# Attention scores of a two-layer hybrid trunk: float32r parts on the whole array, three score banks, stepwise gate products

## The chip, the cores and the metric

The kernel runs on one core of a Trainium2 chip. The metric is the device time of one execution in microseconds (us): the median of three runs, and for the profile the one execution that the hardware profiler recorded. Engines are named as in the profile: PE is TensorE's matmul row and PEld its weight loads, DVE is VectorE, ACT ScalarE, POOL GpSimd, SP SyncE (which only issues transfers).

## What is computed

Two layers work on 2048 latent tokens (a 32 x 64 grid) and 256 context tokens, 1024 wide, all in float32. One layer, cut to what matters here:

```
h   = rms_norm(x) * (1 + scale) + shift
p   = h @ w_in                                  # 3104 columns, split over four groups
a   = gated linear attention, both directions, chunks of 64 (4 heads)
b   = 2-D Fourier mixing @ w_f
c   = windowed attention: 4 query heads, 2 key heads, 3 blocks of 128 + 256 context keys + a sink
d   = neighbourhood attention on the grid: 4 heads, 8 x 16 window with a bias + 256 context keys
y   = concat(group * silu(its gate)) @ w_out
x   = x + gate * y                              # context tokens too, in layer 0
```

For c and d, q and k are normalized per head (c also rotated); scores are q.k over 64 dimensions, plus a mask or bias, then a softmax over local and context keys together.

## The kernel before, in words

The kernel is written for a planner: the program gives instructions in a logical order, with priorities, and the planner puts them on the engines' queues by its own costs; every queue then runs in order. Tokens come in 9 subs of 256 (sub 0 is context), and tiles of 128.

*Projections* (`project`, `mm3`). A float32 product is made of three float32r products: both operands are split into a high part, which is the value rounded to float32r, and a low part, the rest. One projection of a sub to 256 columns is 2 x 8 x 3 matmuls of 128 x 256. Weights are loaded by SP (L211) and split by ACT (L212) and DVE or POOL (L213). `norm_x` and `prep_h` do the same for the tokens; `norm_x` uses the PSUM bank `ph` for two small matmuls.

*q and k* (`normrope`, `store_t`). For the chunks cq, dq, dk (four heads) and ckv (two heads of k) the projection is squared (L358), multiplied by the norm's weight out of PSUM (L362), scaled and for the window heads rotated, transposed by TensorE into the bank `ph` (L327), copied out by ACT and stored to scratch in HBM, float32, with the 64 dimensions as rows.

*GLA* (`gla_fast`) runs beside the projections; its score tile for four heads is read out as 2, 1 and 1 heads. Its outputs use the bank `py`.

*Attention* (`attention`, `pipeline`, `swa`, `na`, `na_ctx_rows`). The work is a list of items, one for each head and block of 128 queries: 272 items in the two layers (176 with 640 keys, 64 with 768, 32 shorter). `load_q` brings q from scratch by SP, twice, once to rows 0 to 63 and once to rows 64 to 127 (four slots), since in `attend` the local keys lie on rows 0 to 63 and the context keys on rows 64 to 127, each multiplied on its half of the array in float32 (L816). The scores of one item fill the only tile of the pool `pS`, two PSUM banks. One DVE instruction adds the bias or mask, stores the negated scores and takes their extremum (L822); ACT takes the exponential and its sum (L830); `transpose_p` transposes blocks of 128 keys by TensorE into one of the two banks of `pm` (L848), DVE copies the first three blocks out (L858) and ACT the rest (L856); L908 multiplies by the values for a pair of heads into `py`, and DVE multiplies by the reciprocal sums (L911). Two small copies on POOL belong to it: the sink column behind the scores (L826) and the reciprocal sums of a pair, spread over columns for a transpose (L851). The bias of a neighbourhood head comes by SP into one tile for each of the two heads of a pair (L998). Keys come by POOL's queue (`na_keys` and `prep` of `swa`, L1023 to L1027 and L926), five items ahead.

*Output* (`prep_mix`, `out_proj`). A half of a sub's group outputs and its gates (`scr_y`, `scr_g`) are loaded to y (one buffer) and g, multiplied on DVE (L1069), and split (L1070, L1071); out_proj then is 4 x 48 matmuls a sub. In `attention` such a call is an item of its own in the list: when it is reached, the products of all its subs are put at high priority, and the matmuls behind them.

*Banks.* PSUM's eight banks: `pp` two (projections), `pS` two, `pm` two, `py` one, `ph` one.

## Time and profile before

| | us |
|---|---|
| median of 3 runs | 2973.59 |
| lowest, highest | 2966.96, 2979.63 |
| profiled execution | 2984.5 |
| its span, first to last instruction | 2982.7 |
| PE busy in the span | 2727.1 (91%) |
| DVE busy | 1596.8 (54%) |
| ACT busy | 1044.7 (35%) |
| POOL busy | 808.7 (27%) |

Matmuls overlap, so a busy PE is not PE at its peak. Attention lies from about 915 to 1560 us (layer 0) and from 2389 to 2925 us (layer 1); projections and GLA before, with the Fourier mixing and the backward GLA scan between; at the end stand the last output projections.

### The profile page before, as it was taken

What the parts mean: (1) busy time and instruction counts of PE and PEld (TensorE: products, weight loads), DVE (VectorE), ACT (ScalarE), POOL (GpSimd) and SP (SyncE); (2) the same over time, 40 slices, a digit from 0 to 9 for tenths busy, and PEclk for the clock granted to TensorE, in tenths of its full rate; (3) what the DMA queues carried; (4) which work ended last, traced back from release to release, by engine and by line L of the source; (5) the groups of instructions that cost most, each with busy time, mean ns of one, the idle gap of its engine ahead of it and who ended that gap; (6) DMA issues with size and microseconds to landing.
All of it is one profiled execution on the core that took longest, in us unless ns stands there. A gap on an engine that the chain in (4) does not pass through costs nothing. (4 is left out here: it accounts for less than half of the span.)

```text
span 2982.7 us, 55851 instructions
## 1 busy us (share of the span) xinstructions
PE 2727.1 (91%) x21206; PEld 2404.4 (81%) x21206; DVE 1596.8 (54%) x3730; ACT 1044.7 (35%) x2322; POOL 808.7 (27%) x911
## 2 busy tenths in 40 slices
PE   5999999999789989989998998999997988898988
PEld 5989999999767657758787988989986866585868
DVE  7556444587663655453747454346339446545453
ACT  2333342343222543342443333323432235324342
POOL 3234323323441111111413333234126211111212
PEclk9999999999889999999999999999998999899999
DMA  7523443363645735364444465233327475455535
GB/s 248 175 92 101 144 132 92 111 220 122 180 139 162 208 100 173 108 162 140 142 136 154 145 197 170 89 94 127 115 83 209 123 198 157 121 168 150 176 108 161
DMA packets 430921, 434.95 MB, mean 146 GB/s; under 512 B 54059, under 2 KB 309805, under 8 KB 430253
## 3 DMA queue, kind: packets, MB, share of 16 engines
q1 hardware_dynamic: 427022, 417.59, 46.0%
q0 software_dynamic: 3616, 13.64, 1.8%
q8 instruction: 172, 2.82, 0.4%
q14 instruction: 111, 0.91, 0.1%
HBM read 328.03 MB, written 103.07 MB: 145 GB/s over the span
## 5 line engine op out<-in xcount | busy, mean ns | idle before, releaser
L220 PE MATMUL ps<-whi,hh 128*128 128x256 f32 x1968 | 578.4, 294 | 28.7 <-DVE nsq L362 21.7
L222 PE MATMUL ps<-whi,hl 128*128 128x256 f32 x1968 | 572.5, 291 | 6.9 <-DVE hl L259 5.2
L221 PE MATMUL ps<-wlo,hh 128*128 128x256 f32 x1968 | 572.4, 291 | 6.9 <-PEq L625 6.0
L213 POOL TENSOR_TENSOR wlo<-wraw,whi 128x512 fp32r<-128x512 f32 x208 | 283.8, 1364 | 855.4 <-ACT whi L212 828.4
L220 PEld LDWEIGHTS ps<-whi,hh 128*128 128x128 f32 x1968 | 385.5, 196 | 40.9 <-DVE nsq L362 13.8
L212 ACT CAST whi<-wraw 128x512 fp32r<-128x512 f32 x416 | 243.0, 618 | 486.9 <-DMA wraw<-w_in 221.2
L220 PE MATMUL ps<-hh,whi 128*128 128x256 f32 x1376 | 404.0, 294 | 8.9 <-DVE nsq L362 5.9
L221 PE MATMUL ps<-hl,whi 128*128 128x256 f32 x1376 | 399.7, 291 | 0.0
L222 PE MATMUL ps<-hh,wlo 128*128 128x256 f32 x1376 | 398.8, 290 | 0.0
L221 PEld LDWEIGHTS ps<-wlo,hh 128*128 128x128 f32 x1968 | 385.6, 196 | 9.9 <-issue 6.3
L222 PEld LDWEIGHTS ps<-whi,hl 128*128 128x128 f32 x1968 | 385.4, 196 | 9.1 <-DVE hl L259 6.6
L220 PE MATMUL pso<-mh,whi 128*128 128x256 f32 x1088 | 319.0, 294 | 9.5 <-ACT mh L1070 5.8
L222 PE MATMUL pso<-mh,wlo 128*128 128x256 f32 x1088 | 316.7, 292 | 4.0 <-POOL wlo L213 2.8
L221 PE MATMUL pso<-ml,whi 128*128 128x256 f32 x1088 | 316.5, 291 | 0.0
L830 ACT ACTIVATE S<-S,am 128x641 f32<-128x641 f32 (+5 forms) x272 | 226.4, 832 | 190.4 <-DVE am L822 173.0
L816 PE MATMUL pse<-kst,q 64*128 64x256 f32 (+2 forms) x1184 | 257.5, 476 | 36.6 <-DVE am L822 32.6
L213 DVE TENSOR_TENSOR wlo<-wraw,whi 128x512 fp32r<-128x512 f32 x208 | 192.6, 931 | 182.2 <-ACT whi L212 174.5
L848 PE MATMUL ppt<-idn,S 128*128 128x128 f32 x1360 | 237.7, 294 | 54.5 <-DVE pt L858 42.4
L220 PEld LDWEIGHTS ps<-hh,whi 128*128 128x128 f32 x1376 | 269.9, 196 | 16.8 <-DVE nsq L362 7.2
L848 PEld LDWEIGHTS ppt<-idn,S 128*128 128x128 f32 x1360 | 153.9, 146 | 150.5 <-issue 45.7
L222 PEld LDWEIGHTS ps<-hh,wlo 128*128 128x128 f32 x1376 | 269.2, 196 | 5.0 <-issue 4.8
L221 PEld LDWEIGHTS ps<-hl,whi 128*128 128x128 f32 x1376 | 269.6, 196 | 3.2 <-issue 2.7
(200 smaller groups left out, 4817.4 us busy)
## 6 DMA issues: line engine op xcount, KB each, us to landing
wraw<-w_in SPq DMA_DIRECT2D x288, 256.0 KB
wraw<-w_out SPq DMA_DIRECT2D x128, 256.0 KB
adaw<-ada_w SPq DMA_DIRECT2D x82, 256.0 KB
scr_g<-ev SPq DMA_DIRECT2D x68, 256.0 KB
g<-scr_g SPq DMA_DIRECT2D x34, 512.0 KB
y<-scr_y SPq DMA_DIRECT2D x34, 512.0 KB
bias<-nbias SPq DMA_DIRECT2D x48, 256.0 KB
brec<-scr_so SPq DMA_DIRECT2D x34, 321.0 KB
```

The source lines that it names most:

```text
L212: nc.scalar.copy(hi[:, k], raw)
L213: (nc.gpsimd if i % 4 else nc.vector).tensor_tensor(out=lo[:, k], in0=raw, in1=hi[:, k], op=ALU.subtract)
L220: nc.tensor.matmul(out, ah(k), bh(k), start=(k == 0), stop=False)
L221: nc.tensor.matmul(out, ah(k), bl(k), start=False, stop=False)
L222: nc.tensor.matmul(out, al(k), bh(k), start=False, stop=(k == KB - 1))
L816: nc.tensor.matmul(p[:, lo:hi], q[r], k, start=True, stop=True, tile_position=(64 * o, 0))
L830: nc.scalar.activation(out=S[:, 0:w], in_=S[:, 0:w], func=AF.Exp, scale=-1.0, bias=m[:, 0:1], accum_out=m[:, 1:2])
L848: nc.tensor.transpose(p[:, i], S[:, (c0 + i) * 128:(c0 + i + 1) * 128], self.idn)
```

## The change

- `store_t` becomes `split_t`: the transposed q or k is split out of PSUM, the high part by ACT as a rounding copy, the low part by DVE as a subtraction, and both are stored. The transposes now use the bank of `py`; the pool `ph` is gone, and the small matmuls of `norm_x` move to `pm`.
- Keys are loaded with the high part on rows 0 to 63 and the low part on rows 64 to 127, local and context keys alike. q's high part lies on both halves of the rows, and its low part, in another tile, too. A score block is then two float32r matmuls over 128 rows, accumulated: (high q) x (high and low k), (low q) x (high and low k).
- Loads of q and k convert from float32 to float32r and go by POOL's queue. For a pair of neighbourhood heads one transfer brings both parts of both heads, with the 64 source rows read twice; for a block of the window heads there are four.
- The scores of two consecutive heads lie in one tile of three banks: the first head's local keys end at column 512 and its context keys follow, the second head's context keys start at 768 and its local keys at 1024. The order of probability blocks and values of the second head changes with it.
- Two bias tiles for each head of a pair, used in turn.
- In `attention` the gate products of three calls of out_proj are steps behind later items: at each step, two items apart, one half is multiplied and the next is loaded, and out_proj's matmuls follow the last one. A product is pinned behind what is already in DVE's order, and goes into g, not y. The other out_proj calls, and the gate projections, are put behind the last item of the phase ahead of them.
- The copies of the transposed probabilities of a pair's first head are all on DVE, those of the second all on ACT.
- GLA's score tile is read out as 3 heads and 1.

```diff
@@ Kern.build, norm_x
-            self.ph = ctx.enter_context(tc.tile_pool(name="ph", bufs=1, space=PSUM))
...
-        p1 = self.ph.tile([128, 512], F32, tag="h", name="p1")
+        p1 = self.pm.tile([128, 512], F32, tag="m", name="p1")
@@ store_t -> split_t
-        p = self.ph.tile([128, 2, 256], F32, tag="h", name="pst")
+        p = self.py.tile([128, 2, 256], F32, tag="y", name="pst")
...
-        x = self.ev.tile([128, 2, 256], F32, tag="sq", name="th")
+        hi = self.ev.tile([128, 2, 256], F32R, tag="sq", name="th")
+        lo = self.ev.tile([128, 2, 256], F32R, tag="e", name="tl")
...
-            nc.scalar.copy(x[:, 0:n], p[:, 0:n])
+            nc.scalar.copy(hi[:, 0:n], p[:, 0:n])
+            nc.vector.tensor_tensor(out=lo[:, 0:n], in0=p[:, 0:n], in1=hi[:, 0:n], op=ALU.subtract)
+        for l, x in zip(range(2), (hi, lo)):
+            x = x.bitcast(F32)
+            if name == "cq":
+                nc.sync.dma_start(self.sqc[l].rearrange("(i p) t -> p i t", p=128)[:, :, tok], x)
+            elif name == "ckv":
+                nc.sync.dma_start(self.skc[:, l, :, tok], x[:, 0])
+            elif name == "dk":
                 for i in range(2):
+                    nc.sync.dma_start(self.skd[2 * i:2 * i + 2, l, :, tok], x[:, i])
...
@@ gla_fast
-                for h0, n in ((0, 2), (2, 1), (3, 1)):
+                for h0, n in ((0, 3), (3, 1)):
@@ loads
-    def load_q(self, pool, src, n):
-        q = pool.tile([128, n, 128], F32, tag="q", name="q", bufs=4, padded_shape=[128, 4, 128])
-        for o in range(2):
-            self.nc.sync.dma_start(q[64 * o:64 * o + 64], src)
-        return q
+    def load_k(self, pool, dst, src, h0, t0, n):
+        src = src[h0:h0 + 2].rearrange("h l d t -> (l d) h t")
+        self.nc.gpsimd.dma_start(dst[:, :, 0:n], src[:, :, t0:t0 + n])
+    def load_q(self, pool, src):
+        q = pool.tile([128, 2, 2, 128], F32R, tag="q", name="q", bufs=4)
+        self.nc.gpsimd.dma_start(q.rearrange("p h l t -> p (h l t)"), src.rearrange("d h l t -> d (h l t)").rearrange("(o d) x -> o d x", o=1).to_broadcast([2, 64, 512]))
+        return q[:, :, 0], q[:, :, 1]
+    def load_q4(self, pool, src):
+        out = []
+        for d in range(2):
+            q = pool.tile([128, 4, 128], F32R, tag="q", name="q", bufs=4)
+            for o in range(2):
+                self.nc.gpsimd.dma_start(q[64 * o:64 * o + 64], src(d))
+            out.append(q)
+        return out
@@ attend
-        p = self.pS.tile([128, 1024], F32, tag="s", name="pse")
-        for o, lo, hi, k in parts:
-            r = slice(64 * o, 64 * o + 64)
-            nc.tensor.matmul(p[:, lo:hi], q[r], k, start=True, stop=True, tile_position=(64 * o, 0))
+        n, a0 = nloc + 256, 768 if side else 512 - nloc
+        p = self.S3
+        for lo, hi, k in ((1024, 1024 + nloc, kloc), (768, 1024, kc)) if side else ((a0, 512, kloc), (512, 768, kc)):
+            if hi > lo:
+                nc.tensor.matmul(p[:, lo:hi], qa[:, h], k, start=True, stop=False)
+                nc.tensor.matmul(p[:, lo:hi], qb[:, h], k, start=False, stop=True)
@@ transpose_p
-            if c0:
+            if rc is not None:
                 nc.scalar.copy(pt[:, 0:w], p[:, 0:w])
             else:
                 nc.vector.tensor_copy(out=pt[:, 0:w], in_=p[:, 0:w])
@@ kv_tiles (new, in place of na_keys)
+        kc = pool.tile([128, 2, 256], F32R, tag="kc", name="kc", bufs=2)
+        self.load_k(pool, kc, kt, h0, 0, 256)
+        kst = None
+        if n:
+            kst = pool.tile([128, 2, 1024], F32R, tag="kst", name="kst", bufs=2)
+            self.load_k(pool, kst, kt, h0, t0, n)
@@ na
+            b = pool_st["b", i]
             if cg != 2:
-                if ("b", i) not in pool_st:
...
+                b.insert(0, b.pop())
@@ prep_mix
-    def prep_mix(self, L, s):
+    def prep_mix(self, L, subs, late=False):
...
+        def product(s, c):
+            g, y = got.pop(0)
+            hh, hl = mix[s]
+            ins = nc.vector.tensor_tensor(out=g, in0=y, in1=g, op=ALU.mult)
+            if late:
+                self.tc.keep_in_program_order(ins)
+            nc.scalar.copy(hh[:, :, c], g)
+            (nc.gpsimd if c.start else nc.vector).tensor_tensor(out=hl[:, :, c], in0=g, in1=hh[:, :, c], op=ALU.subtract)
...
+        def step(k):
+            if k > 0:
+                product(*halves[k - 1])
+            if k < len(halves):
+                load(*halves[k])
@@ attention
+            self.S3 = self.pS.tile([128, 1536], F32, tag="s", name="pse")
+            for i in range(2):
+                self.bias["b", i] = [p.tile([128, 768], F32, name=f"bias{i}{x}", bufs=1) for x in range(2)]
...
+                n = 2 * len(subs)
+                for k in range(1, n + 1):
+                    behind.setdefault(at + 2 * k, []).append(lambda k=k: out.steps[k]())
+                behind.setdefault(at + 2 * n, []).append(lambda: self.out_proj(L, subs, mix))
@@ trunk
-                self.attention(L, 3, 2, g, [10, 11, 12, 13, 14, 15], 0, f(T3), [-2, -1, 0, 1, 2, 3], None, 1, f(T1), [4, 5, 6, 7, 8, 9])
+                self.attention(L, 3, 2, g, [10, 11, 12, 13, 14, 15], 0, ("out", T3), [-2, -1, 0, 1, 2, 3], None, 1, ("out", T1), [4, 5, 6, 7, 8, 9])
...
-                self.attention(L, 3, 2, g, [10, 11, 12, 13, 14, 15], 0, f(T3), [0, 1, 2, 3], 1, [4, 5], [6, 7], [8, 9], f(T1), f([3, 4]), f([5]))
+                self.attention(L, 3, 2, g, [10, 11, 12, 13, 14, 15], 0, ("out", T3), [0, 1, 2, 3], 1, [4, 5], [6, 7], [8, 9], f(T1), f([3, 4]), f([5]))
```

## Rows read from the trace of the kernel before

**Rows 1.** Page: busy us of each engine, share of the span, instructions.

```profile
PE 2727.1 (91%) x21206; PEld 2404.4 (81%) x21206; DVE 1596.8 (54%) x3730; ACT 1044.7 (35%) x2322; POOL 808.7 (27%) x911
```

**Rows 2.** Windows by stage: start:end, length, busy us of each engine, PEclk, DMA share, GB/s.

```profile
100.00:750.00 650.00, 632.76 (x5027) 606.36 (x5026) 368.25 (x829) 227.26 (x492) 201.79 (x164) 0.99 0.43 136
915.00:1560.00 645.00, 587.92 (x4753) 465.76 (x4751) 336.22 (x829) 247.66 (x592) 122.42 (x232) 0.95 0.51 147
1560.00:2250.00 690.00, 650.32 (x5090) 623.70 (x5089) 339.95 (x733) 238.37 (x498) 224.04 (x182) 0.98 0.43 135
2389.00:2925.00 536.00, 483.72 (x3959) 372.78 (x3958) 277.81 (x673) 214.24 (x513) 91.61 (x188) 0.94 0.54 154
```

**Rows 3.** Page: the chain that ended last, shares of the span by line.

```profile
PE py L908 2%; PE pse L816 2%; PE ppt L848 2%; DMA y<-scr_y 2%; PE pso L220 2%; PE pso L222 1%; PE pso L221 1%; DMA bias<-nbias 1%; DMA wraw<-w_out 1%; DMA scr_y<-yt 1%; ACT S L830 1%; DVE S L822 1%; PE pab L726 1%; PE ps L220 1%; PE ps L22
```

**Rows 4.** Waits of the whole span: engine and line <- releaser, us in total, times, longest.

```profile
DVE y L1069 <- DMA y<-scr_y: 84.7, 29, 8.6
...
PE ppt L848 <- DVE pt L858: 42.4, 15, 5.7
...
POOL kst L1023 <- PE pse L816: 36.5, 10, 6.4
...
PE pse L816 <- DVE am L822: 32.6, 61, 3.9
...
PE ps L220 <- DVE nsq L362: 27.7, 18, 6.9
...
DVE S L822 <- DMA bias<-nbias: 22.3, 10, 5.3
```

**Rows 5.** Timeline of three short stretches, TensorE: start us, us, engine, line, operation, tiles.

```profile
2639.51 0.30 PEld L816 LDWEIGHTS pse<-kst,q 64*128 64x128 f32 x4 [0.17 <-issue]
2639.52 0.91 PE L816 MATMUL pse<-kst,q 64*128 64x384 f32 x4
...
2640.36 0.77 PE L848 MATMUL ppt<-idn,S 128*128 128x128 f32 x5
...
2780.65 0.93 PE L816 MATMUL pse<-kst,q 64*128 64x384 f32 x6
...
2781.50 0.33 PE L852 MATMUL ppt<-idn,rd 128*128 128x128 f32 x1
...
2783.08 0.28 PE L220 MATMUL pso<-mh,whi 128*128 128x256 f32 x1
...
2783.20 0.28 PE L221 MATMUL pso<-ml,whi 128*128 128x256 f32 x1
```

**Rows 6.** Timeline around a gate product, TensorE and then VectorE.

```profile
2516.84 0.91 PE L816 MATMUL pse<-kst,q 64*128 64x384 f32 x4 [0.29 <-DVE am L822]
...
2519.61 0.91 PE L816 MATMUL pse<-kst,q 64*128 64x384 f32 x4
...
2523.33 0.43 PE L848 MATMUL ppt<-idn,S 128*128 128x128 f32 x2 [2.33 <-DVE pt L858]
...
2521.38 1.23 DVE L1069 TENSOR_TENSOR y<-y,g 128x1024 f32<-128x1024 f32 x1 [2.31 <-DMA y<-scr_y]
```

**Rows 7.** Groups by line and shape, whole span: busy us, mean ns, idle before.

```profile
L822 DVE CUSTOM_DVE_ANT_0 S<-pse,cmask,sink 128x640 f32<-128x640 f32 x112 | 98.5, 880 | 40.9 <-PE pse L816 28.7 <-issue 6.2 <-POOL S L826 2.6
...
L421 PE MATMUL pu<-av,ktt 128*128 128x256 f32 x144 | 40.1, 401 | 3.3 <-ACT ktt L418 3.3
...
L726 PE MATMUL pab<-XT,G 128*128 128x512 f32 x64 | 29.4, 602 | 0.0
...
L362 DVE TENSOR_TENSOR nsq<-ps,wdk 128x512 f32<-128x512 f32 x18 | 12.2, 681 | 0.0
...
L1023 POOL DMA_DIRECT2D kst<-scr_kd x18 | 11.1, 614 | 73.2 <-PE pse L816 36.5 <-DVE ev L279 26.7 <-PE ppt L852 7.8
...
L362 DVE TENSOR_TENSOR nsq<-ps,wck 128x256 f32<-128x256 f32 x18 | 7.5, 415 | 0.0
```

**Rows 8.** DMA issues: tiles, queue, count, KB each, median us to landing.

```profile
kst<-scr_kd POOLq DMA_DIRECT2D x16, 384.0 KB, 5.6
...
kst<-scr_kd POOLq DMA_DIRECT2D x26, 128.0 KB, 4.0
```

More of the change, by code (lines that the diff above doesn't have):

```diff
@@ L1175, in attention, with wrap, last @@
                 elif isinstance(ph, tuple):
-                    items.append((None, lambda: None, lambda r, x, f=ph[1]: x == 2 and f()))
-                elif ph:
+                    out(ph[1], len(items) - 1)
+                elif callable(ph):
+                    behind.setdefault(len(items) - 1, []).append(ph)
+                else:
                     items += self.swa(L, p, ph)
-            self.pipeline(items)
+            def wrap(i, item):
+                prep, front, back = item
+                def last(r, x):
+                    back(r, x)
+                    if x == 2:
+                        for f in behind.pop(i, []):
+                            f()
+                return prep, front, last
+            self.pipeline([wrap(i, it) for i, it in enumerate(items)])
+            for i in sorted(behind):
+                for f in behind[i]:
+                    f()
     def trunk(self):
```

185 lines of the change are left out of this document (92 added, 93 removed).

## The prediction

> **What bounds the kernel now.** I read the page's busy lines first, to see which engine could set the time [rows 1]: TensorE is busy 2727.1 of 2982.7 us, VectorE only 1596.8. TensorE's queue is in order, so the time is its work plus the places where its next instruction waits. The windows by stage [rows 2] show where that happens. In the two stretches of projection work (100 to 750 and 1560 to 2250 us) TensorE stands idle 17 and 40 us. In the two attention stretches (915 to 1560 and 2389 to 2925, together 1181 us) it stands idle 57 and 52 us, and the granted clock drops to 0.95 and 0.94. What the change does happens mostly in those 1181 us.
>
> The chain [rows 3] is made of small pieces of many lines, so no single line is the bound. The table of waits [rows 4] names what stops an engine: TensorE's scores (L816) for VectorE's read of the previous scores, 32.6 us; its transposes (L848) for a VectorE copy, 42.4 us in 15 waits of up to 5.7; VectorE's gate product (L1069) for its y tile, 84.7 us; its score read for a bias, 22.3 us. One stretch of the timeline [rows 6] joins the second with the third: at 2521.38 VectorE starts a gate product after 2.31 us of waiting for y, and TensorE's transposes, whose bank is emptied by a copy queued behind that product, start 2.33 us late at 2523.33. So a waiting gate product is paid for by TensorE.
>
> **The score matmuls.** Before, a head's scores are float32 on 64 rows of the array, the local and context keys on different halves. From the first score matmul to the next instruction TensorE spends 0.84 us for 640 keys (2639.52 to 2640.36) and 0.85 us for 768 (2780.65 to 2781.50) [rows 5]. After, each block of keys is streamed twice in float32r on all 128 rows. The projections show that pace: 0.12 us from one 128x256 float32r matmul to the next (2783.08 to 2783.20) [rows 5]. The trace has no float32r matmul of 384 or 512 columns. The float32 ones [rows 7] grow with the columns (401 ns at 256, 602 at 512), so I take 0.18 and 0.24 us in proportion. A head then costs 2 x (0.18 + 0.12) = 0.60 us for 640 keys and 2 x (0.24 + 0.12) = 0.72 for 768. By the loops there are 176 heads of 640, 64 of 768 and 32 shorter ones (I give them 0.3 us each): 176 x 0.24 + 64 x 0.13 + 32 x 0.3 = 42 + 8 + 10 = 60 us. If a 384 block cost as much as a 512 one, the first term is 176 x 0.12 = 21 and the sum 39. If the 0.17 us that the weight row waits before a score group [rows 5] is TensorE's own loss and goes too, it is 60 + 272 x 0.1 = 87. I take 60, since the pace is steady in its row.
>
> **Three banks.** The scores of the next head may be written while VectorE still reads (0.88 us, L822) [rows 7]. But both heads' context columns lie in the middle bank, so only the local part (0.36 of 0.60 us) is certainly free of the wait. I take 20 of the 32.6 us; bounds 0 and 33. The Trainium skill (PSUM — Partial Sum Buffer, section "PSUM bank collisions raise a hardware error") says to guard PSUM by bank, not by address: another column of a bank that is being read still collides. That rule speaks against counting the whole wait; by it, the context pass still waits for the read, and the sum would take about 0.36/0.60 of the wait; the rows alone allow all of it. No row of before shows two heads in one bank.
>
> **Gate products.** Three of the calls of out_proj (both of layer 0's attention, the first of layer 1's) load a half two items ahead of its product and pin the product's place in VectorE's queue: 18 of the 34 halves. Their share of the 42.4 us is 18/34, or 22; I take 20 of bounds 0 and 42. What comes late instead is out_proj: for three subs its matmuls start 12 items after the attention that feeds them, and until then less dense work fills TensorE's gaps. I charge 5 us, 0 to 30. The product now goes into g, so y's only buffer is free after the product, not after the two splits behind it; the 16 halves outside gain a little, counted in the bounds.
>
> **Second bias buffer.** Removes a 22.3 us wait of VectorE [rows 4]. VectorE is busy 614 of the 1181 us [rows 2], so most of that was cover: 5 us, bounds 0 and 22.
>
> **Clock.** Of the two levels 2.4 and 1.2 GHz, a mean of 0.95 over 645 and 0.94 over 536 us means 65 + 64 us at 1.2 [rows 2]; work done there takes twice the time. They are the stages in which TensorE also stands longest. If a third of the standing goes, I let a part of this go too: 10 us, bounds 0 and 40.
>
> Sum of gains: 60 + 20 + 20 + 5 + 10 = 115 us.
>
> **What is added.** The split of q and k into two parts adds a VectorE subtraction from PSUM to each of 52 projections of four heads and 18 of two; by L362, which reads the same shapes, 52 x 0.68 + 18 x 0.415 = 43 us [rows 7]. It falls in the projection stretches, where VectorE is busy 708 of 1340 us and TensorE has a 128x256 product about every 0.12 us to hide it. TensorE waits there 27.7 us for VectorE's L362 to free a projection bank [rows 4]; a longer queue adds to that: 10 us, bounds 0 (all hidden) and 43 (none).
>
> The bank ph goes. Its transposes now share the one bank of the GLA and attention outputs, and now hold it through ACT's copy and the subtraction; norm_x moves into the two banks of the attention transposes. The holds are short and TensorE has other work there: 10 us, bounds 0 and 40.
>
> q moves from SP's queue to POOL's: 4 transfers for each of 34 blocks, and one for each of 68 pairs, 204 at 0.61 us of POOL each [rows 7], 125 us on an engine busy 214 of the 1181 us [rows 2]. Behind a q transfer that waits for its slot stand the copies L851 and L826 and the weight splits L213, as they stand behind L1023 now (36.5 us of waits) [rows 4]. Four q slots hold two blocks now, not four. I charge 10 us, bounds 0 and 100. SP loses 204 issues and gains 157 for the doubled stores; no row has it on the path, so nothing either way; if stores did delay weight loads it would show in L212's wait. The larger score copies of the GLA (3 heads and 1, not 2, 1 and 1) save an instruction on ACT and VectorE, off the path: nothing. The other moves (the copies of one head all on VectorE, of the other all on ACT) keep the load of a pair.
>
> Costs: 5 + 10 + 10 + 10 = 35 us. Net: 115 - 35 = 80 us faster. The profiled execution took 2984.5 us, 1.8 more than its span; it becomes 2904.5. It lay 11 above the median of the three runs, 2973.6, so on that scale I predict 2973.6 - 80 = 2893 us. Half a per cent, 15 us, is about what can be told from no change.
>
> **Rivals.** *Only the matmul work goes.* The attention stages turn out to be paced by the round of a head (scores, read, exp, transposes, copies), and the removed waits come back as others at the same places. Then 60 less the costs remain: 25 us, 2949. For it: the waits are spread over many pairs [rows 4] and the chain passes through all engines [rows 3]. Against: rows 6 show a wait whose cause is removed.
>
> *The costs take it all*: 2973.6 give or take 15. This is the case if the splits and shared banks cost near their upper bounds, 43 and 40.
>
> *Slower: q comes late.* The one load of a pair reads its 64 rows twice, through a repeated outer dimension of two, and is converted on the way. If that spreads it over few engines, its landing grows. Over all engines 128 KB land in 4.0 us and 384 KB in 5.6 [rows 8], so 256 KB cost 1.6 us of moving; on two of sixteen, eight times that, 13 us, plus a base of some 3. Where nothing fills the gaps, heads follow each other 2.8 us apart (2516.84 to 2519.61) [rows 6], after the change perhaps 2.5; with three pairs of two heads ahead of the one in use the room is 15 us, and past that each of the 64 pairs waits a third of the rest. Against a gain of 90 without the 10 charged for q it decides from a landing of 19 us (64 x 1.3 = 85); 20 us gives 2990, 25 gives 3097, say 3020. For it: nothing in the trace has this shape. Against: the loads can start early, and the room is larger where projection work lies between. The Trainium skill (DMA: Bandwidth & Descriptors, section "Rules for kernel authors") says that a leading zero-stride broadcast of c copies confines a DMA to at most c engines; by it q's load would run on two. No run here shows it yet; by rows 8 even then the landing of 16 lies near the room, so I give it a modest chance.
>
> **Chances.** Forecast (up to 2930) 0.62, of which 0.06 below 2835, where several gains reach their upper bounds; only the matmul work (2930 to 2958) 0.13; costs take all (2959 to 2988) 0.11; q late or another new wait, over 2988, 0.14. So faster 0.75, same 0.11, slower 0.14. The range 2835 to 2988 leaves out the first 0.06 and the last 0.14.
>
> **What would show it.** A 640-key score group 0.60 us from its start to the next instruction; VectorE's wait for y shorter by half or more; no wait of some 2 us at L848 behind a gate product; a bias wait near zero; attention stages together near 1090 us at a granted clock not below 0.95; projection stretches longer by 10 to 30 us. Wrong it would be made by VectorE or ACT waiting for a q transfer, TensorE idle in the 12 items before a late out_proj, or projections that wait for the output bank.

## The result, and the profile after

The changed kernel took 3273.8 us (median of four runs, 3264.7 to 3280.8) against 2972.7 before on the same chip: ratio 1.101, 95% interval 1.097 to 1.105. The forecast was 2893, and 2835 to 2988 the range; the change made the kernel 301 us slower. The profiled execution has a span of 3262.9 us and a granted clock of 0.915 (before 2982.7 and 0.960).

The busy line of the page, beside [rows 1]:

```profile
PE 2734.1 (84%) x21078; PEld 2528.3 (77%) x21078; DVE 1629.7 (50%) x3790; ACT 1064.7 (33%) x2312; POOL 944.3 (29%) x1111
```

TensorE is busy 2734.1 us, as before (2727.1). What grew is its standing: 3262.9 - 2734.1 = 529 us against 2982.7 - 2727.1 = 256. So 273 of the 280 us by which the span grew are time in which TensorE waits. That its busy time didn't fall is a loss too: the kernel combo3, below, runs the same 21078 matmuls in 2657.7 us, at a granted clock of 0.956.

Windows whose bounds are the first and last score matmul of each layer tell where (columns as in [rows 2]). First come two of the kernel before, the projections ahead of layer 0's scores and those between the layers:

```profile
100.00:921.00 821.00, 775.32 (x5904) 730.72 (x5904) 471.01 (x1089) 268.12 (x584) 270.16 (x224) 0.97 0.45 140
...
1532.00:2394.00 862.00, 802.10 (x6119) 758.61 (x6119) 439.14 (x977) 281.23 (x592) 287.60 (x237) 0.97 0.45 140
```

then all four of the changed kernel:

```profile
100.00:1064.00 964.00, 799.56 (x5740) 741.75 (x5738) 488.72 (x1115) 263.30 (x564) 270.09 (x228) 0.90 0.42 129
1064.00:1622.00 558.00, 488.34 (x4190) 437.81 (x4190) 279.45 (x733) 235.09 (x558) 167.37 (x299) 0.95 0.72 172
1622.00:2670.00 1048.00, 861.68 (x6279) 808.12 (x6278) 497.16 (x1081) 294.72 (x606) 304.21 (x264) 0.89 0.43 130
2670.00:3185.00 515.00, 449.95 (x3901) 410.03 (x3900) 268.01 (x663) 222.28 (x509) 156.42 (x271) 0.94 0.74 184
```

Layer 0's attention became shorter (558 us; before 611, from 921 to 1532), layer 1's stayed (515 and 515). The two projection stages grew by 143 and 186 us, and there TensorE's standing went from 46 to 164 us and from 60 to 186; the clock granted fell from 0.97 to 0.90 and 0.89, so that a share of the work that is left ran at 1.2 GHz and not at 2.4. The larger part of the loss is not where the change was aimed, but where q and k are made.

The waits of the whole span, beside [rows 4]:

```profile
PE ps L219 <- DVE nsq L371: 77.0, 33, 7.0
...
ACT ev L299 <- DMA scr_kd<-tl: 69.6, 6, 13.8
...
PE pse L840 <- DVE am L847: 62.6, 85, 10.6
DVE g L1095 <- DMA y<-scr_y: 61.3, 19, 10.4
...
PE ps L219 <- ACT ev L299: 52.5, 9, 13.3
...
DVE tl L339 <- DMA scr_kd<-tl: 47.9, 6, 10.5
...
PE p L239 <- DVE rb L238: 42.6, 12, 9.1
...
DVE S L847 <- DMA bias<-nbias: 14.9, 7, 3.8
...
PE ppt L873 <- DVE pt L883: 11.5, 9, 5.1
```

In these rows th and tl are the tiles of the high and the low part. The gate product's wait for y (84.7 before), the transposes' wait for VectorE's copy (42.4) and the bias's (22.3) all fell, as meant, though the first by a quarter and not by the half that the prediction named as a sign. New ones stand above them: ScalarE and VectorE wait for the store of the keys' low part, up to 13.8 us at a time, and TensorE waits for ScalarE's evacuation (L299) behind it. One such place, in the timeline of all engines (L351 stores keys, L299 evacuates a projection, L219 is the next projection's first matmul):

```profile
1784.33 1.84 SPq L351 DMA_DIRECT2D scr_kd<-th  x1
...
1789.39 0.63 ACT L338 CAST th<-pst 128x256 fp32r<-128x256 f32 x1 [6.95 <-DVE tl L339]
...
1789.85 0.28 PE L221 MATMUL ps<-whi,hl 128*128 128x256 f32 x1
...
1790.63 3.84 SPq L351 DMA_DIRECT2D scr_kd<-tl  x2
...
1794.52 2.59 SPq L302 DMA_DIRECT2D scr_vd<-ev  x1
...
1802.75 1.13 ACT L299 COPY ev<-ps 128x512 f32<-128x512 f32 x2 [12.25 <-DMA scr_kd<-tl]
...
1803.39 0.58 PE L219 MATMUL ps<-whi,hh 128*128 128x256 f32 x1 [13.27 <-ACT ev L299]
```

TensorE's last matmul starts at 1789.85 and the next at 1803.39: the evacuation had no buffer until a store had landed, and the store's two issues took SyncE 2.22 and 1.53 us (the keys' store was one issue of 0.37 us before).

In the attention the score groups came out near the forecast. The timeline of TensorE at one 640-key head:

```profile
1118.62 0.34 PE L840 MATMUL pse<-kst,q 128*128 128x384 f32 x1
1118.80 0.34 PE L841 MATMUL pse<-kst,q 128*128 128x384 f32 x1
1118.97 0.28 PE L840 MATMUL pse<-kc,q 128*128 128x256 f32 x1
1119.09 0.28 PE L841 MATMUL pse<-kc,q 128*128 128x256 f32 x1
1119.21 0.27 PE L873 MATMUL ppt<-idn,S 128*128 128x128 f32 x1
```

0.59 us from the first to the next instruction (0.84 in [rows 5]; forecast 0.60); the pair's other head, at 1123.83, takes 0.70.

### The profile page after: what moved, and what is told of

Its sections match the earlier page's. It is cut to its first block, busy times and chain, and to the rows that moved or that the text cites. A ratio compares the mean times of both kernels' runs of the same rounds, so it can differ in the third digit from the quotient of the medians.

```text
span 3262.9 us, 56102 instructions
## 1 busy us (share of the span) xinstructions
PE 2734.1 (84%) x21078; PEld 2528.3 (77%) x21078; DVE 1629.7 (50%) x3790; ACT 1064.7 (33%) x2312; POOL 944.3 (29%) x1111
## 5 line engine op out<-in xcount | busy, mean ns | idle before, releaser
L219 PE MATMUL ps<-whi,hh 128*128 128x256 f32 x1968 | 600.1, 305 | 116.7 <-ACT ev L299 52.5
L221 PE MATMUL ps<-whi,hl 128*128 128x256 f32 x1968 | 593.4, 302 | 14.6 <-DVE hl L258 14.6
L220 PE MATMUL ps<-wlo,hh 128*128 128x256 f32 x1968 | 591.3, 300 | 1.9 <-POOL wlo L212 1.9
L212 POOL TENSOR_TENSOR wlo<-wraw,whi 128x512 fp32r<-128x512 f32 x208 | 274.1, 1318 | 1075.3 <-ACT whi L211 1042.3
L219 PEld LDWEIGHTS ps<-whi,hh 128*128 128x128 f32 x1968 | 408.1, 207 | 130.6 <-ACT ev L299 54.5
L211 ACT CAST whi<-wraw 128x512 fp32r<-128x512 f32 x416 | 242.6, 619 | 625.7 <-DMA wraw<-w_in 263.6
L219 PE MATMUL ps<-hh,whi 128*128 128x256 f32 x1376 | 401.8, 292 | 32.7 <-DVE nsq L371 25.4
L221 PEld LDWEIGHTS ps<-whi,hl 128*128 128x128 f32 x1968 | 407.8, 207 | 18.4 <-DVE hl L258 16.7
L220 PEld LDWEIGHTS ps<-wlo,hh 128*128 128x128 f32 x1968 | 409.0, 208 | 3.7 <-POOL wlo L212 2.3
L212 DVE TENSOR_TENSOR wlo<-wraw,whi 128x512 fp32r<-128x512 f32 x208 | 184.7, 891 | 292.1 <-ACT whi L211 290.4
L219 PE MATMUL pso<-mh,whi 128*128 128x256 f32 x1088 | 314.9, 290 | 7.3 <-DVE xo L1131 4.4
L219 PEld LDWEIGHTS ps<-hh,whi 128*128 128x128 f32 x1376 | 271.1, 197 | 37.0 <-ACT whi L211 11.6
L873 PE MATMUL ppt<-idn,S 128*128 128x128 f32 x1360 | 229.4, 285 | 39.7 <-ACT pt L881 14.4
L190 POOL TENSOR_TENSOR rs<-ms,mhalf 128x4 f32<-128x4 f32 (+2 forms) x140 | 168.8, 1207 | 321.8 <-DVE ms L188 306.8
L219 PEld LDWEIGHTS pso<-mh,whi 128*128 128x128 f32 x1088 | 213.4, 197 | 10.1 <-DVE xo L1131 4.4
## 6 DMA issues: line engine op xcount, KB each, us to landing
q<-scr_qd POOLq DMA_DIRECT2D x64, 256.0 KB, 12.1
```

What stands on the lines that cost most here:

```text
L190: nc.gpsimd.tensor_tensor(out=rs, in0=ms, in1=self.mhalf.to_broadcast([128, n]), op=ALU.pow)
L211: nc.scalar.copy(hi[:, k], raw)
L212: (nc.gpsimd if i % 4 else nc.vector).tensor_tensor(out=lo[:, k], in0=raw, in1=hi[:, k], op=ALU.subtract)
L219: nc.tensor.matmul(out, ah(k), bh(k), start=(k == 0), stop=False)
L220: nc.tensor.matmul(out, ah(k), bl(k), start=False, stop=False)
L221: nc.tensor.matmul(out, al(k), bh(k), start=False, stop=(k == KB - 1))
```

## The experiments

The kernel before was timed beside each of them (2972.7 to 2982.7 us), so they are set against one another by their ratios to it, a difference of ratios (with their fourth digit) taken times 2973 us. The table has all kernels; the last five columns are, from each trace (one execution), the time to layer 0's first score matmul, from there to its last, to layer 1's first, to its last, and the tail behind it.

| kernel | median us | ratio to before (95%) | to scores | attention 0 | between | attention 1 | tail |
|---|---|---|---|---|---|---|---|
| before | 2973 | 1 | 921 | 611 | 862 | 515 | 74 |
| changed | 3273.8 | 1.101 (1.097 to 1.105) | 1064 | 558 | 1048 | 515 | 78 |
| k_rows | 3213.7 | 1.080 (1.076 to 1.083) | 1020 | 588 | 1004 | 527 | 76 |
| q_two | 3202.5 | 1.077 (1.074 to 1.080) | 1054 | 531 | 1043 | 491 | 76 |
| ph_back | 3128.0 | 1.051 (1.048 to 1.054) | 1028 | 542 | 987 | 496 | 78 |
| b_dk2 | 3022.2 | 1.017 (1.014 to 1.020) | 937 | 608 | 886 | 515 | 71 |
| combo3 | 2978.4 | 0.998 (0.996 to 1.000) | 961 | 539 | 923 | 476 | 77 |
| two_banks | 3324.2 | 1.116 (1.111 to 1.121) | 1092 | 563 | 1071 | 512 | 78 |
| pst_ph | 3175.1 | 1.063 (1.060 to 1.066) | 1022 | 541 | 1048 | 489 | 79 |
| pst_m | 3353.7 | 1.123 (1.120 to 1.127) | 1113 | 568 | 1069 | 525 | 76 |
| combo3_at_once | 3018.0 | 1.013 (1.011 to 1.016) | 957 | 586 | 897 | 500 | 78 |
| scoped3 | 2998.3 | 1.007 (1.005 to 1.009) | 960 | 526 | 960 | 471 | 77 |
| scoped3_at_once | 3036.6 | 1.019 (1.017 to 1.021) | 963 | 539 | 957 | 498 | 79 |
| combo3_no_tl | 2947.5 | 0.990 (0.987 to 0.992) | 941 | 539 | 920 | 472 | 75 |
| combo3_sq3 | 2957.6 | 0.993 (0.991 to 0.995) | 938 | 546 | 915 | 480 | 75 |
| combo3_vrows | 2936.9 | 0.986 (0.984 to 0.988) | 940 | 533 | 907 | 482 | 74 |
| b_vrows | 2976.4 | 1.000 (0.998 to 1.002) | 930 | 601 | 861 | 511 | 72 |
| best | 2935.4 | 0.986 (0.984 to 0.989) | 939 | 541 | 903 | 479 | 76 |
| after_sq3 | 3277.7 | 1.100 (1.097 to 1.104) | 1072 | 572 | 1054 | 510 | 77 |
| b_dk2_vrows | 2990.3 | 1.003 (1.002 to 1.005) | 934 | 607 | 874 | 501 | 72 |

Late output projections lie between the attention stages in the changed kernels, and inside them before, so for those the two middle columns are read together. In general the stages don't hold the same work: the planner orders the whole program anew for each kernel. Attention 0 has 4482 matmuls before, 4190 in the changed kernel, 3967 in combo3 and 3883 in scoped3, and a projection's matmul takes some 0.12 us, so a hundred of them move a bound by 12 us. Where it matters, TensorE's standing is given beside the length.

Standing is not all that differs. These kernels run the same 21078 matmuls, and TensorE's busy time in them is: two_banks 2784.1 us (granted clock 0.903), changed 2734.1 (0.915), pst_ph 2711.8 (0.932), ph_back 2702.9 (0.935), combo3 2657.7 (0.956), best 2657.5 (0.958). From two_banks to ph_back the span falls by 185 us, of which 104 are standing and 81 busy time at the lower clock. So the prices below hold both; no run changes one without the other.

### Which part costs: keys' store, queries' load, banks

**Keys' store (k_rows).** The key scratch gets the part as its outermost dimension, each part is stored as one transfer, and each key load becomes two of 64 rows:

```
-  nc.sync.dma_start(self.skd[2 * i:2 * i + 2, l, :, tok], x[:, i])     # for i in range(2)
+  nc.sync.dma_start(self.skd[l].rearrange("(i h) d t -> (h d) i t", i=2)[:, :, tok], x)
```

> The changed kernel, with the key scratch laid out part first, so that the neighbourhood keys' store is one transfer of 128 x 2 x 256 for each part (as the kernel before had it, twice), where the changed kernel has two transfers whose outermost dimension has only 2 entries; the sliding window's key store likewise; the price is that each key load becomes two transfers of 64 rows. Theory A (those stores crawl: they back up SyncE's queue behind which weights wait, and hold the evacuation buffers): the store's issue goes back from 0.76 us to about 0.4 us, the waits of ScalarE and VectorE for the store of the key scratch (69.6 + 47.9 + 21.8 us) go under 15 us together, and the time falls by 120 to 250 us, to 3020 to 3150. Rival B (the shared PSUM banks stall the projections): the waits for the stores go, but TensorE then waits for the banks, and the time falls by under 40 us. Rival C (the attention's queries are late): no change in the projections' part is worth more than 40 us.

Measured: 64 us won (1.101 - 1.080). Half of the least that theory A wanted, more than B or C allowed. The issue went to 0.37 us, ScalarE's wait for the store of the low part fell from 69.6 to 21.4 us, and VectorE's from 47.9 to none that is listed; A wanted under 15 for all. The 64 us are net: the two projection stages became 88 us shorter, and the two attention stages, where each key load is now two transfers, 42 us longer, with 45 us more of standing.

**Queries' load (q_two).**

```
-  src ... .rearrange("(o d) x -> o d x", o=1).to_broadcast([2, 64, 512])   # one load
+  for o in range(2): self.nc.gpsimd.dma_start(q[64 * o:64 * o + 64], src)
```

> The changed kernel, with the pair's queries loaded by two transfers of 64 rows of 2 KB in place of one whose outermost dimension is a repeat of 2. Rival C (the repeated query load lands late, 12 us at the median, and fills few engines): the landing falls to 4 to 6 us, and the time falls by 60 us or more, to under 3215. Theory A (the key stores) and rival B (the banks): the time stays within 30 us of 3274, for the attention stages had already become shorter.

Measured: 72 us won, as theory C wanted; A's and B's "within 30" fell. The DMA issues of the changed kernel, then of this one (tiles, queue, count, KB each, median us to landing):

```profile
q<-scr_qd POOLq DMA_DIRECT2D x64, 256.0 KB, 12.1
```

```profile
q<-scr_qd POOLq DMA_DIRECT2D x128, 128.0 KB, 4.8
```

The repeated load took 12.1 us, with a longest of 24.8. TensorE's wait for it is listed with only 11.5 us, but the two attention stages, with nearly the same matmuls in them (4187 and 3875; 4190 and 3901 in the changed kernel), became 51 us shorter, and TensorE stands 31 us less there. By which rows the rest of the 72 went isn't shown. The Trainium skill (DMA: Bandwidth & Descriptors, section "Rules for kernel authors") advises against an outermost dimension under 16, a repeat among them; the landing in this pair of rows agrees, though how many engines the load ran on isn't in them.

**Banks (ph_back).** The fourth small bank comes back for transposes (pst) and the norm's columns (p1); scores and the linear attention go back to two banks and groups of 2, 1, 1 heads.

> The changed kernel, with the PSUM bank for transposes and the norm's columns taken back out of the three score banks: scores in two banks, both heads of a pair in the same place, the linear attention's scores in groups of 2, 1, 1 heads. Rival B (shared banks): TensorE's wait of the projections for VectorE's reduction (77 us, 27.7 before) goes back to about 30, and the time falls by 40 us or more. Theory A (key stores): within 30 us of the changed kernel either way, where the attention loses what the third score bank gave, some 20 us by the prediction's term.

Measured: 149 us won, the largest of the three, and more than B asked, though the wait that B named (77.0 us) went to 59.9 and not to about 30. Three further kernels take it apart:

```
   two_banks: two score banks, pst and p1 in the shared banks, one bank unused
   pst_ph:    as ph_back, but p1 stays in the shared two-buffer bank
   pst_m:     the changed kernel, pst in the shared two-buffer bank, not in the outputs' bank
```

> The changed kernel with scores in two banks and the linear attention's groups of 2, 1, 1 heads as before, but the transposes and the norm's columns still in the shared banks, so that one PSUM bank lies unused. Theory F (the sharing costs, not the third score bank): 3274 plus what the third bank gave, 3270 to 3310. Rival G (the loss is in what the three-bank tile does to the linear attention and to the Fourier head, whose matmuls share that one buffer): near 3128, as with the bank given back.

> As the kernel with the fourth small bank back, but only the transposes of the projections are in it; the norm's columns stay in the two-buffer bank. Theory F1 (the transposes in the one-buffer bank of the linear attention's outputs are what costs): near 3128, under 3160. Rival F2 (the norm's columns in the two-buffer bank are what costs): over 3230.

> The changed kernel, with the transposes of the projections in the two-buffer bank and not in the one-buffer bank of the linear attention's outputs; three score banks stay. Theory F1: 60 us or more are won, to under 3215, for the linear attention's output no longer takes turns with the transposes. Rival F3 (any sharing costs, since every bank's next owner waits for an evacuation that stands behind a stalled engine): within 30 us of 3274.

Measured: with two score banks and the sharing left, 45 us slower than the changed kernel (outside F's range, on its side; G is out). So sharing costs 1.116 - 1.051, 194 us: 158 of them by the transposes (1.116 - 1.063; the kernel's 3175 us lie between what F1 and F2 wanted, nearer F1) and 36 by the norm's columns. F1's reason is not right: in the other shared bank, which has two buffers, the transposes cost 67 us more, and TensorE's wait for VectorE's product out of a projection's bank (nsq) is 135.0 us there (77.0 in the changed kernel). Rival F3's words fit better, though not its number: any sharing costs. What the transposes do to the others is in the view of tile pst, idle time of the engines ahead of its instructions, by what ended it; two_banks and then ph_back:

```profile
  PE pst L326: 220.7, 45
  ACT th L341: 91.8, 27
  ACT th L338: 80.5, 26
```

```profile
  PE pst L327: 111.5, 36
  ACT th L339: 74.4, 26
  ACT th L342: 48.6, 19
```

ScalarE stands 220.7 us until a transpose has been made when its bank is shared, 111.5 when it has one of its own (223.4 in the changed kernel, 82.2 before). VectorE, whose subtraction needs ScalarE's cast, stands 172.3 and 123.0. Both are in-order, and the evacuations that free TensorE's other banks stand behind. TensorE itself is listed with 4.4 and 2.7 us of standing ahead of the transposes, so they don't wait at the head of its queue: they come late in it, in the order that the planner made. What falls at TensorE when the transposes get their bank (two_banks to pst_ph) is the wait for nsq, from 80.6 to 41.5 us; the wait for the norm's row (L239) falls from 48.4 to 38.3, and to 13.7 when the norm's columns move too. That the one leads to the other is read from the queues, not shown by a run of its own, and no run keeps the order and changes the bank alone: two_banks also has 232 and 256 more matmuls in its attention stages than pst_ph.

**The three mends together (combo3).**

> The changed kernel with all three mends together: the key scratch part first (60 us by itself), the pair's queries in two transfers (71 us), the fourth small PSUM bank back and scores in two banks (146 us). Theory D (three separate losses, of different places, that add): 3274 - 60 - 71 - 146 = 2997, between 2980 and 3020. Rival E (they share a cause, SyncE's and GpSimd's queues with the late weights behind them, so that the second mend finds less to win): over 3050.

Measured: ratio 0.998, so 306 us are won back, where the three alone give 64 + 72 + 149 = 285. They add (theory D, whose range ends at 2980; 2978 was measured), and a little more. E is out. The loss of 301 us is accounted for by these three edits; but the kernel is only level with the one before. Its attention stages are 72 and 39 us shorter, but part of that is output projections that now lie between them, and the projection stages are 40 and 61 us longer.

### Why the stores cost

**One such store in the kernel before (b_dk2).**

```
-  nc.sync.dma_start(self.skd.rearrange("(i h) d t -> (h d) i t", i=2)[:, :, tok], x)
+  for i in range(2): nc.sync.dma_start(self.skd[2 * i:2 * i + 2, 0, :, tok], x[:, i])
```

> The kernel before, with one thing of the change: the neighbourhood keys' store in two transfers whose outermost dimension has 2 entries (the two heads), in place of one of 128 x 2 x 256; still one part of the keys, so half the bytes of the changed kernel. Theory A: such a store lands in 8 us or more where it took 2 to 4, and the time rises by 40 to 200 us. Rivals B and C, and the forecast's step that stores lie on no path: within 10 us of 2973.

Measured: 50 us slower, with the same bytes. Theory A's time holds; the landing that it named isn't listed in the trace. The changed kernel's timeline shows how it goes. Here are rows of SyncE in one projection chunk (start, us; x6 are six issues together, with the waits between them):

```profile
490.41 0.49 SPq L351 DMA_DIRECT2D scr_kd<-th  x1
...
520.54 1.69 SPq L351 DMA_DIRECT2D scr_kd<-tl  x1
522.28 16.32 SPq L305 DMA_DIRECT2D scr_vd<-ev  x6
538.70 10.75 SPq L210 DMA_DIRECT2D wraw<-w_in  x4
```

Taken one by one, the issues in such a chunk are of two kinds. Some take SyncE 0.33 to 0.7 us; others, behind the two-slice stores, 1.1 to 3.1. The six of the values' store take 2.61, 2.63, 0.49, 1.73, 0.49 and 1.76 us; the rest of their 16.32 is waiting for evacuated tiles. The four weight loads behind them take 2.54, 0.38, 0.38 and 0.33, and the last of the four waits from 542.2 to 549.1, for one of their three buffers. So the weights come out last, and ScalarE waits for them. The window 520 to 540 of the same kernel says what the DMA engines do meanwhile (the last two columns are their share and GB/s):

```profile
520.00:540.00 20.00, 13.71 (x98) 13.50 (x97) 2.63 (x3) 2.81 (x6) 1.29 (x1) 0.83 0.14 49
```

A share of 0.14, about two of sixteen engines, and 49 GB/s. The Trainium skill (DMA: Bandwidth & Descriptors, section "Why a DMA increments its semaphore by 16 and not by 1") says that a transfer runs on the largest number of engines up to 16 that divides the slowest dimension of both its patterns, here 2; this window agrees. The values' store (vd, L305) has the same form, two of the four column residues outermost, in the kernel before as well. So it was tried too:

```
-  for t in range(2): nc.sync.dma_start(dst.rearrange("(c r) d -> r c d", r=4)[2 * t:2 * t + 2], e[:, t])
+  for r in range(4): nc.sync.dma_start(dst.rearrange("(c r) d -> r c d", r=4)[r], e[64 * (r % 2):64 * (r % 2) + 64, r // 2])
```

> The kernel with the three mends, with the neighbourhood values' store, which in both kernels is two transfers with an outermost dimension of 2, in four transfers of 64 rows of 1 KB. If it is the outermost 2 that makes a store slow (45 us for the keys' 36 such stores in the kernel before): 20 to 45 us less than 2978. Rival: within 6 us, since only a wait of 10.5 us for these stores is in the trace.

> The kernel before, with the neighbourhood values' store in four transfers of 64 rows of 1 KB in place of two with an outermost dimension of 2. If the outermost 2 makes a store slow: 20 to 45 us less than 2978. Rival: within 6 us, since only a wait of 5.0 us for these stores is in the trace.

Measured: 36 us won in the kernel with the mends (0.998 - 0.986), nothing in the kernel before (1.000). The first expectation held, the second fell to its rival. And with the keys' slow store put into the kernel before:

> The kernel before, with the keys' store in two transfers with an outermost dimension of 2, which cost 45 us, and with the values' store, which follows it, in 64-row transfers. If the slow stores cost only where the two kinds queue up behind one another: back near 2978, under 2990. Rival (the keys' store costs by itself, through the transposed tile that waits for it): 3010 or more.

Measured: 1.003 where the keys' store alone gave 1.017, so 40 of the 50 us go when the values' store is made quick, though the keys' slow store stays (2990.3 us, at the edge of the expectation). ScalarE's wait for weights goes with the time; the kernel before, b_dk2 and b_dk2_vrows:

```profile
ACT whi L212 <- DMA wraw<-w_in: 221.2, 81, 13.4
```

```profile
ACT whi L212 <- DMA wraw<-w_in: 270.3, 84, 17.4
```

```profile
ACT whi L212 <- DMA wraw<-w_in: 225.9, 80, 12.6
```

The other way in which a slow store could cost, the tile that it holds, doesn't go with it: ScalarE's wait for the keys' store is 20.2 us in b_dk2 and still 19.3 in b_dk2_vrows. And the values' store, whose form b_dk2 leaves alone, takes SyncE 2.32 us at the median there, 0.51 in the kernel before. So it is mostly the queue of several slow stores with the weights behind it that costs, not a store by itself. The same chunk in six kernels, from the first keys' store to the end of the last weight issue, waits included:

| kernel | keys' store | values' store | SyncE from, to | length |
|---|---|---|---|---|
| changed | slow, both parts | slow | 490.41 to 549.45 | 59.0 |
| b_dk2 | slow, one part | slow | 449.56 to 494.79 | 45.2 |
| combo3 | quick, both parts | slow | 450.02 to 490.45 | 40.4 |
| before | quick, one part | slow | 441.13 to 477.16 | 36.0 |
| b_dk2_vrows | slow, one part | quick | 445.88 to 480.64 | 34.8 |
| best | quick, both parts | quick | 445.35 to 476.83 | 31.5 |

In this stretch the kernel before has TensorE busy 34.92 of 36.20 us, so there the queue is covered and shortening it wins nothing; combo3 has 35.97 of 40.50, the changed kernel 41.55 of 59.10 at a granted clock of 0.85:

```profile
490.40:549.50 59.10, 41.55 (x299) 39.73 (x297) 16.10 (x30) 13.21 (x31) 8.60 (x7) 0.85 0.23 74
```

One chunk of six is shown; that the others go alike is not.

### Buffers of the low part, and the split itself

```
   sq3:    the low part tl from the squares' ring, now of three buffers, not from the evacuations' two ("e");
           for the room, one buffer fewer of the reciprocals' rows
   no_tl:  lo = hi, the two subtractions and tl's buffer removed
```

> The changed kernel, with nothing but the low part moved into the squares' ring of three buffers. If the slow key stores cost mainly because they hold a buffer that the projections evacuate into: 50 us or more less than 3274. Rival (what costs is SyncE's queue behind the slow stores, and the shared banks): within 25 us of 3274.

> The kernel with the three mends, with the low part moved out of the two buffers of the projections' evacuations into the ring of the squares, which gets a third buffer (one copy of the reciprocals' rows is given up for the room). If the shared two buffers hold the projections up: 10 to 30 us less than 2978. Rival: within 6 us, the buffers come free in time since the stores are quick again.

> The kernel with the three mends, without the low part of queries and keys: VectorE's subtraction and its buffer are gone, and the high part is stored twice, so that scores are made of the high parts alone. It gives what the split itself costs; the prediction's term was 10 us with bounds 0 and 43. Theory H (the split's place on VectorE and the evacuation buffers is what is still missing before the attention, 961 us against 921): 20 to 43 us less, 2935 to 2958, most of it ahead of the first attention. Rival I (the doubled stores and loads, which stay here, or a later start of the attention): within 10 us of 2978.

Measured: on the changed kernel the ring alone is worth nothing (1.100), as its rival said; ScalarE's cast of the high part then waits 56.9 us for the keys' store instead. With the mends it is worth 16 us (0.998 - 0.993), and leaving the split out 26 (0.998 - 0.990), most of it ahead of the scores (961 to 941). Theory H, in its lower half.

### Gate products and the third bank

**Products at once (combo3_at_once).** The two kinds of phase that step the products become plain calls again:

```
-  self.attention(L, 3, 2, g, [...], 0, ("out", T3), ...)
+  self.attention(L, 3, 2, g, [...], 0, f(T3), ...)
```

> The kernel with the three mends, but the late output projections make their gate products all at once, as the kernel before did. The prediction's term for the stepwise products was 20 us (bounds 0 and 42), with 5 us against it for the later start. If the term holds: 2978 + 15 = 2993, and VectorE's wait for the attention outputs' load (71.4 us in the kernel with the three mends) goes back to 85 or more. Rival: the time stays within 6 us of 2978, since the products' stalls only moved.

Measured: 45 us slower (1.013 - 0.998), where 15 were expected. The term holds and was too small. The waits, at once and then stepwise:

```profile
DVE g L1097 <- DMA y<-scr_y: 100.9, 26, 10.6
...
PE ppt L875 <- DVE pt L885: 39.3, 18, 10.7
```

```profile
DVE g L1097 <- DMA y<-scr_y: 71.4, 20, 8.0
...
PE ppt L875 <- DVE pt L885: 17.5, 11, 7.6
```

VectorE waits 29.5 us less for y, and TensorE's transposes 21.8 less for VectorE. The late output projections move work from attention 0 to the stretch behind it: 586 + 897 at once, 539 + 923 stepwise.

**Banks by stage (scoped3).** Two score banks and the small bank outside the attention, three score banks inside it; scoped3_at_once has the products at once as well.

> The kernel with the three mends, with the eight PSUM banks dealt by stage: the fourth small bank and two score banks outside the attention, three score banks inside it, where neither the transposes nor the norm's columns run. By the two kernels without the small bank, 3324 us with two score banks and 3274 with three, the third bank is worth 50 us in the attention: 2978 - 50 = 2928, between 2910 and 2950. Rival: the 50 us came from the linear attention's groups of three heads, or the hand-over of the banks between stages costs as much as it gives: 2965 or more.

> Banks dealt by stage as in the last kernel, and the gate products all at once. With both terms: 15 us slower than that kernel. Rival: within 6 us of it, or faster, if the later start of the late projections costs more than the stepwise products give.

Measured: 27 us slower than combo3. The attention stages are 13 and 5 us shorter, but they also hold 84 and 9 fewer matmuls, and TensorE stands 73 and 60 us in them, 73 and 65 in combo3; so in the attention the third bank is worth some 5 us of standing, in one execution of each. The stretch between the layers, where the banks are handed back, grows by 37 us and holds 90 more matmuls. The rival's time (2965 or more) holds; of its two reasons the hand-over fits, but the moved work is part of it. The 45 us of the third bank in the changed kernel (two_banks to changed) lie in the projection stages, 28 and 23 us, where the linear attention then takes three heads at a time, and hardly in the attention (5 and -3). They aren't standing, which is 532 and 529 us: 50 of the 53 us between the two spans are busy time, at the clocks given above. With the products at once another 35 us are lost (15 expected).

### The best version

This is combo3 with both further edits (sq3 and vrows).

> The kernel with the three mends, with both further edits: the low part in the squares' ring of three buffers (20 us less by itself) and the values' store in 64-row transfers (41 us less by itself). If the slow store costs because its buffer is one that the low part waits for, either edit cures most of it and they don't add: 2925 to 2940. If they are separate: 2978 - 20 - 41 = 2917, between 2908 and 2924. Either way the fastest of all kernels here.

Measured: 2935.4, ratio 0.986 (0.984 to 0.989): 41 us faster than the kernel before, and no faster than with the values' store alone. The two edits don't add, so the ring mended what the slow values' store did. The same windows of this kernel as were shown of the changed one:

```profile
100.00:939.00 839.00, 790.23 (x5985) 744.28 (x5984) 494.55 (x1142) 272.27 (x594) 274.24 (x236) 0.96 0.51 151
939.00:1480.00 541.00, 471.72 (x4037) 419.50 (x4038) 291.32 (x760) 235.65 (x556) 194.73 (x365) 0.94 0.78 176
1480.00:2383.00 903.00, 845.12 (x6466) 800.77 (x6464) 490.65 (x1068) 295.76 (x624) 301.33 (x260) 0.96 0.51 151
2383.00:2862.00 479.00, 416.67 (x3628) 373.66 (x3629) 261.01 (x655) 215.56 (x498) 171.37 (x321) 0.95 0.87 194
```

TensorE stands 49 and 58 us in the projection stages, as before (46 and 60), and 69 and 62 in the attention (55 and 52 there before, in longer stages). Over the whole span TensorE is busy 70 us less than before (2657.5; 2727.1) at nearly the same clock, and stands 25 us more. What was won is matmul work; the attention still waits, and more than it did.

## Why the prediction was wrong, step by step

**The step that failed** is the list of what is added, in three of its terms, with 10 us for each of two and none for the third; mended together, with the third score bank given back, they are worth 306.

- *"SP loses 204 issues and gains 157 for the doubled stores; no row has it on the path, so nothing either way."* It counted issues and not what the issues carry. The store of a pair of heads has 2 as its outermost dimension, and it stands ahead of the weights in SyncE's queue. It cost 64 us. The prediction asked what an outermost dimension of 2 does to the queries' load, where it is a repeat, and not to the stores, where it is written as a slice. The sign it named, a longer wait in L212's place, came: ScalarE's cast waits for weights 263.6 us, 221.2 before.
- *"The holds are short and TensorE has other work there: 10 us, bounds 0 and 40."* Sharing cost 194 us, 158 of it by the transposes. The term looked for a wait of TensorE at the bank, and there is nearly none (4 us). What grew is ScalarE's standing until the transposes, which then came late in TensorE's queue, had been made: 223.4 us, 82.2 before; and TensorE waited for evacuations behind it.
- *"I charge 10 us, bounds 0 and 100"* for the queries: 72, within the bounds. The rival for it expected a landing of 16 us and put the point of decision at 19; the landing was 12.1 at the median, and it already cost near the 85 us that the rival gave at 19. So the room of three pairs of two heads that it reckoned with can't have been there; no run measures it.
- The split: 26 us with its buffer, charged 10, within its bounds of 0 and 43. The wait that it was to lengthen (27.7 us, for VectorE's product out of the projection's bank) is 77.0 in the changed kernel, but 36.1 in combo3 and 14.4 in best, so most of that growth isn't the split's.

**Gains.** Score matmuls: a head takes 0.59 and 0.70 us, where 0.60 was said for both; the steps of 0.12 and 0.18 us are in the rows. No run has them alone; the 70 us that TensorE is busy less in best than before are near the 60 forecast. Three banks: 20 said; some 5 us of standing by stage, and 45 in the changed kernel, but as busy time in the projections. TensorE's wait for VectorE's read, which the gain was to come from, rose from 32.6 us to 62.6 (50.4 with two banks and the mends, 47.1 with three), so it is luck that the 20 lie between. Gate products: 45 us net, where 20 less 5 was said; the term was mis-sized, since it counted 18 of 34 halves of one wait and nothing of what stands behind. Bias: the wait fell from 22.3 to 14.9, and no run prices it. Clock: 10 us were to be gained, and it went the other way, from 0.960 to 0.915, in the kernel in which TensorE stood 273 us longer; against combo3 at 0.956, the same matmuls took 76 us more of busy time.

**Rivals.** The one on the other side (q late) was a quarter of the loss. "Costs take all", with splits and shared banks near 43 and 40, named the right place for the largest part, the shared banks, with a fifth of its size (40 against 194). With the losses mended and the third bank given up, the change is worth 41 us (the values' store adds nothing to the kernel before), near the rival "only the matmul work goes" (25) and under the forecast's 80.

**What stays open.** Why the transposes cost even more in the two-buffer bank; how much of the banks' price is the sharing itself and how much the order that the planner then makes; why the stretch between the layers grows by 37 us when the banks are dealt by stage; what share of each price is the clock; and the price of the low part's subtraction apart from its stores, which the run without it leaves in.

## What to carry to other kernels

Read the outermost dimension of both sides of each new transfer, stores too, and ask what stands behind it in its queue: several transfers of two slices in a row held back weights that had nothing to do with them. A PSUM bank is worth the standing of all who wait for its next owner; before one is taken from a stage, count the in-order engines that evacuate it there, not only the time for which it is held. And a slow transfer may cost nothing until its cover is used up: the same store was free in one kernel and 36 us in the other.

## What the runs showed of the hardware that was not expected

A DMA issue on SyncE isn't of a fixed price: 0.33 to 0.5 us as a rule, and 1.1 to 3.1 us for many that stand behind two-slice stores. It falls on whoever comes next: in b_dk2 the values' store went from 0.51 us to 2.32 at the median by the keys' store ahead of it, and in the changed kernel the first weight load behind the stores took 2.54 us, the next two 0.38 each. The kernel before has it too (2.51 us for the first weight load behind the values' store of the same chunk), best hardly (0.53). While such stores run the DMA engines move 49 GB/s at a share of 0.14.
